# Sparse attention: softmax weights left unscaled, head outputs scaled by reciprocal sums that go through DRAM

## The chip, the cores and the metric

The kernel runs on one core of one Trainium2 chip, as one launch. The metric is the device time of that launch in microseconds. TensorE is PE in the rows below (its weight loads PEld), VectorE is DVE, ScalarE is ACT, GpSimd is POOL, and SyncE is SP, which issues nearly all DMAs in the order in which they stand in its queue. Every engine works through its own instructions in a fixed order and waits on semaphores of the others.

## What is computed

One decoder layer on 512 tokens of width 1024, and a final RMSNorm. Two branches read the same normed input: sparse attention with 16 heads of 64, and a Mamba-2 scan. Both are gated and merged, and a gated MLP follows. The change is in the attention branch, whose core is, for each block of 128 queries:

```python
c_sel = gather(c_kv, sel)                       # the 128 keys that an indexer selected
logits = einsum("bqhc,bqkc->bhqk", qb, c_sel) * scale + bias[t5_bucket(dist)]
p = softmax(where(dist >= 0, logits, -inf), axis=-1)
out = einsum("bhqk,bqkc->bqhc", p, c_sel)       # later, per head:
att = einsum("bshc,hdc->bshd", out, w_uv)
y_att = att.reshape(b, s, 1024) @ w_att_out
```

The kernel doesn't gather: a mask `msk` of 0 and a very negative number picks the selected keys, and all causal keys are computed. A softmax row is exp(logit - max) divided by the sum of its exps. The division may be done on the weights, or on the output of the weighted sum, since it is one number per query and head.

## The kernel before

All tensors stay in SBUF, 128 partitions wide. A float32 matrix is split into a rounded part (`hi`, written by ACT, `split` and L86) and the rest (`lo`, a subtraction, L87), and a product is three matmuls. Weights come as tiles `wr` of 128x1024 through `fetch` (two buffers), ACT makes `wh`, POOL makes `wl` (three buffers each).

The attention stage runs from about 440 to 640 us. Its loop (L852) goes over heads h = 0 to 17. In one turn it emits, for head h, four logit steps `lg(i)`, one per block of 128 queries, with one to four blocks of keys (L764); for head h-2 the product with V (`pav_`); for head h-1 the transposes of its weights (`ptrans`); then the softmax of head h (`soft`). Between these steps `weave` lays the projections as filling work for PE: `pq` and `pk` (query and key of the next pair of heads) in even turns, `pgs` (a gate) in odd ones, and every fourth head the values `pV`. Heads go in pairs, p = h // 2, since two heads of 64 fill 128 partitions.

The steps that matter here, with what they run on:

- `logits` (L743): SP loads `T`, a table of the head's position bias, 128x256 (L748, two buffers). POOL adds it to the mask into `bm` (one buffer): L752, the wide L753, twice L759. So POOL can write `bm` of head h only when DVE has read that of head h-1 in its last logit step.
- `lg(i)`: PE multiplies into a PSUM bank `pl`; DVE adds `bm` and takes the row maximum `mx` (L769).
- `soft`: DVE negates `mx` (L773), ACT computes four exps with their sums `sm` (L776), DVE takes the reciprocal of `sm` (L778) and multiplies the weights `pr` by it, block by block (L781).
- `ptrans`: PE transposes ten blocks of `pr` into three banks `pPT`; ACT writes `PTh` (L800), DVE `PTl` (L801).
- `pav_`: eight matmuls into a bank `pav`. The main part of the product is in the 64 rows `r`, a small part in the other 64, `o_`. ACT copies the small part into `hi` of the pair's tile (L821, named `ath`), SP moves it to the right rows of `lo` (L822, `atl`), DVE copies the main part into `cr` (L823, one buffer per pair).
- `att_split(p)` (L825): adds both parts (L829) and splits the sum into `ath` and `atl` of the pair, for the projection `pao`. The add and the subtraction run on POOL for pairs 0 to 5 and on DVE for pairs 6 and 7.

The banks of `pl`, `pav`, `pPT`, `pV` come from one ring of four PSUM banks (`cht`): a new one waits until the fourth before it has been read. The order in each engine's queue is set by a scheduler of the framework from the emitted program; PE's is close to the emitted order, while ACT, DVE, POOL and SP are ordered by when it expects their inputs. After the loop the kernel goes on with `pga` (another gate) and `pao` (the output projection of attention) by turns, 24 matmuls each, then the rest of the layer, which nothing of the change touches.

Of the kernel before, what the change touches and what calls it, by code (L numbers as in the profile page):

```python
# [9 lines left out]
F32 = mybir.dt.float32  # L10
R32 = mybir.dt.float32r
AF = mybir.ActivationFunctionType
OP = mybir.AluOpType

P = 128
S = 512
NB = S // P
D = 1024
KD = D // P
H = 16  # L20
# [9 lines left out]
SEG = (0, 128, 512, 896)  # L30
# [18 lines left out]
def _body(ctx, tc, x, prm_d, cst_d, nfin_d, wI_d, wX_d, wSO_d, wQ_d, wG_d, wAO_d, wO_d, wUp_d, wDn_d,  # L49
          wkv_d, out):  # L50
    nc = tc.nc
# [6 lines left out]
    dram = enter(tc.tile_pool(name="dram", bufs=1, space=bass.MemoryType.DRAM))  # L58
# [6 lines left out]
    def cht(name):  # L65
        return pc.tile([P, 512], F32, tag="ch", name=name)

    def f(t):
        return t.bitcast(F32)
# [12 lines left out]
    ident = cv("ident")  # L82

    def split(hi, lo, src, lo_eng=None):

        nc.scalar.activation(hi, src, AF.Copy)  # L86
        (lo_eng or nc.vector).tensor_tensor(lo, src, f(hi), OP.subtract)  # L87
# [232 lines left out]
    for t in range(4):  # L320
# [3 lines left out]
        for hh in range(2):  # L324
            h = 2 * t + hh
# [366 lines left out]
            split(hi, lo, raw, lo_eng=nc.gpsimd)  # L692
            wkv.append((hi, lo))

    qTs, kTs, Vs, prs, PTs = {}, {}, {}, {}, {}
    KOF = (0, 512, 1024, 896)

    def v_step(qd):
# [44 lines left out]
    def logits(h):  # L743
        p, hh = h // 2, h % 2
        qh, ql = qTs[p][hh]
        kt = kTs[p][hh]
        T = ap_.tile([P, 256], F32, tag="T", name=f"T{h}")
        nc.sync.dma_start(T, bass.AP(tensor=skD.tensor, offset=skD.offset + h * P * UW + 127,  # L748
                                     ap=[[UW - 1, P], [1, 256]]))
        bm = ap_.tile([P, SEGW], F32, tag="bm", name=f"bm{h}", bufs=1)  # L750
        r31 = pv("r31", h, h + 1)
        nc.gpsimd.tensor_tensor(bm[:, 0:P], msk[:, 0:P], T[:, P:], OP.add)  # L752
        nc.gpsimd.tensor_tensor(  # L753
            bass.AP(tensor=bm.tensor, offset=bm.offset + P, ap=[bm.ap[0], [512, 3], [1, 256]]),
            bass.AP(tensor=msk.tensor, offset=msk.offset + P, ap=[msk.ap[0], [512, 3], [1, 256]]),
            T.unsqueeze(1).to_broadcast([P, 3, 256]), OP.add)
        for i in (2, 3):
            o, n = SEG[i], (i - 1) * P
            nc.gpsimd.tensor_tensor(bm[:, o:o + n], msk[:, o:o + n], r31.to_broadcast([P, n]), OP.add)  # L759
        pr = ap_.tile([P, SEGW], F32, tag="pr", name=f"pr{h}")  # L760
        mx = ap_.tile([P, NB], F32, tag="mx", name=f"mx{h}")
        sm = ap_.tile([P, NB], F32, tag="sm", name=f"sm{h}")

        def lg(i):  # L764
            o, n = SEG[i], (i + 1) * P
            pl_ = cht(f"pl{h}_{i}")[:, :n]
            nc.tensor.matmul(pl_, qh[:, i * P:(i + 1) * P], kt[:, :n], start=True, stop=False)
            nc.tensor.matmul(pl_, ql[:, i * P:(i + 1) * P], kt[:, :n], start=False, stop=True)
            nc.vector.tensor_tensor_reduce(pr[:, o:o + n], pl_, bm[:, o:o + n], 1.0, -3e38, OP.add, OP.max,  # L769
                                           mx[:, i:i + 1])  # L770

        def soft():
            nc.vector.tensor_scalar(mx, mx, -1.0, None, OP.mult)  # L773
            for i in range(NB):
                o, n = SEG[i], (i + 1) * P
                nc.scalar.activation(pr[:, o:o + n], pr[:, o:o + n], AF.Exp, bias=mx[:, i:i + 1],  # L776
                                     accum_out=sm[:, i:i + 1])
            nc.vector.reciprocal(sm, sm)  # L778
            for i in range(NB):
                o, n = SEG[i], (i + 1) * P  # L780
                nc.vector.tensor_scalar(pr[:, o:o + n], pr[:, o:o + n], sm[:, i:i + 1], None, OP.mult)  # L781
            prs[h] = pr

        return [lambda i=i: lg(i) for i in range(NB)] + [soft]

    def ptrans(h):
        pr = prs[h]
        PT = (ap_.tile([P, 1280], R32, tag="PTh", name=f"PTh{h}", bufs=1),
              ap_.tile([P, 1280], R32, tag="PTl", name=f"PTl{h}", bufs=1))
        PTs[h] = PT  # L790

        def one(bk, kbs):
            pt = cht(f"pPT{h}_{bk}")
            w = 0
            for kb in kbs:
                for i in range(kb, NB):
                    nc.tensor.transpose(pt[:, w:w + P], pr[:, SEG[i] + kb * P:SEG[i] + (kb + 1) * P], ident)
                    w += P
            o = KOF[kbs[0]]
            nc.scalar.activation(PT[0][:, o:o + w], pt[:, :w], AF.Copy)  # L800
            nc.vector.tensor_tensor(PT[1][:, o:o + w], pt[:, :w], f(PT[0][:, o:o + w]), OP.subtract)  # L801

        return [lambda a=a: one(*a) for a in enumerate(((0,), (1, 3), (2,)))]

    crs = {}

    def pav_(h):

        p, hh = h // 2, h % 2
        r, o_ = slice(64 * hh, 64 * hh + 64), slice(64 - 64 * hh, 128 - 64 * hh)  # L810
        V, PT = Vs[p // 2], PTs[h]
        pav = cht(f"pav{h}")
        for i in range(2):
            for kb in range(NB):
                o = KOF[kb]
                nc.tensor.matmul(pav[:, kb * P:], V[:, kb, h % 4, :], PT[i][:, o:o + S - kb * P],
                                 start=(kb == 0 and i == 0), stop=(kb == NB - 1 and i == 1))
        hi, lo = attT[p]
        if hh == 0:
            crs[p] = ap_.tile([P, S], F32, tag="cr", name=f"cr{p}", bufs=1)  # L820
        nc.scalar.activation(hi[o_], pav[o_], AF.Copy)  # L821
        nc.sync.dma_start(f(lo[r]), f(hi[o_]))  # L822
        nc.vector.tensor_copy(crs[p][r], pav[r])  # L823

    def att_split(p):  # L825
        hi, lo = attT[p]
        s_ = crs[p]
        eng = nc.vector if p >= 6 else nc.gpsimd
        eng.tensor_tensor(s_, s_, f(lo), OP.add)  # L829
        split(hi, lo, s_, lo_eng=eng)  # L830

    sds.close()
# [19 lines left out]
    for h in range(H + 2):  # L852
        p = h // 2
        fl = []
        if h == 2:
            open_att()
        if h < 2:
            hg = len(gs[0]) // 2
            fl = [so[6 + h]] + gs[0][h * hg:(h + 1) * hg]
        elif h < H:  # L860
            if h % 2 == 0 and p + 1 < 8:
                fl = list(qn[p + 1])
            elif h % 2 == 1:
                fl = list(gs[p])
        chain = []
        lg = logits(h) if h < H else []
        chain += [(i < 3, s_) for i, s_ in enumerate(lg[:NB])]
        if h >= 2:
            chain.append((0, lambda: pav_(h - 2)))
        if 1 <= h <= H:  # L870
            chain += [(i == 1, s_) for i, s_ in enumerate(ptrans(h - 1))]
        if h % 4 == 1 and h < H:
            chain.append((0, v_step(h // 4)))
        chain += [(1, s_) for s_ in lg[NB:]]
        if h >= 5 and h % 2 == 1:
            chain.append((0, lambda: att_split((h - 5) // 2)))
        weave(chain, fl)
# [230 lines left out]
```

## Time and profile before

| what | value |
|---|---|
| median of 3 runs | 1142.02 us (1140.78 to 1142.1) |
| profiled execution, own time | 1139.67 us |
| its span (first to last instruction) | 1137.9 us |
| PE busy | 1094.5 us, 96% of the span |
| DVE busy | 669.2 us, 59% |
| ACT busy | 589.3 us, 52% |
| POOL busy | 504.5 us, 44% |
| granted TensorE clock | 0.995 of full speed (the upper of its two levels, 2.4 GHz) |

PE is busy nearly everywhere, so the span falls only where PE waits or where its work shrinks. Busy shares are means over stages with different limits; the attention stage has to be read by itself. The profiled execution took 1139.67 us, of which 1.8 us lie around the span; it is 2.35 us below the median of the runs.

### The profile page before, as it was taken

What the parts mean: (1) busy time and instruction counts of PE and PEld (TensorE: products, weight loads), DVE (VectorE), ACT (ScalarE), POOL (GpSimd) and SP (SyncE); (2) the same over time, 40 slices, a digit from 0 to 9 for tenths busy, and PEclk for the clock granted to TensorE, in tenths of its full rate; (3) what the DMA queues carried; (4) which work ended last, traced back from release to release, by engine and by line L of the source; (5) the groups of instructions that cost most, each with busy time, mean ns of one, the idle gap of its engine ahead of it and who ended that gap; (6) DMA issues with size and microseconds to landing.
All of it is one profiled execution on the core that took longest, in us unless ns stands there. A gap on an engine that the chain in (4) does not pass through costs nothing.

```text
span 1137.9 us, 14581 instructions
## 1 busy us (share of the span) xinstructions
PE 1094.5 (96%) x5268; PEld 906.7 (80%) x5268; DVE 669.2 (59%) x1340; ACT 589.3 (52%) x948; POOL 504.5 (44%) x279
## 2 busy tenths in 40 slices
PE   5999999999999999899998999999999999999997
PEld 5777778788888887787887888878888888888885
DVE  4589999995696894578889433135344343420004
ACT  5364776687767654366766432244444444431223
POOL 3424334344344345666664344443444444444442
PEclk9999999999999999999999999999999999999999
DMA  5464322323322314434433233323322232223321
GB/s 195 122 192 142 117 93 88 102 91 110 102 94 93 130 58 121 137 89 125 126 98 93 84 130 111 112 84 104 110 93 93 95 108 94 93 93 95 107 96 74
DMA packets 43305, 122.06 MB, mean 107 GB/s; under 512 B 5392, under 2 KB 9760, under 8 KB 43232
## 3 DMA queue, kind: packets, MB, share of 16 engines
q1 hardware_dynamic: 42656, 120.07, 33.2%
q8 instruction: 42, 0.69, 0.2%
q10 hardware_dynamic: 576, 1.05, 0.2%
q14 instruction: 31, 0.25, 0.1%
HBM read 108.29 MB, written 5.32 MB: 100 GB/s over the span
## 4 chain that ended last, share of the span: by engine, by line
PE 66%; DVE 19%; ACT 4%; POOL 3%; issue 3%; DMA 1%; POOLq 0%; DVEq 0%; ACTq 0%
PE pup L112 21%; PE pdn L969 10%; PE pxbc L389 6%; PE pso L480 5%; PE pao L112 4%; PE pga L112 4%; PE pwo L913 4%; DVE msk L349 2%; DVE m L348 2%; DVE u L404 2%; DVE pr L781 2%; DVE pr L769 2%; ACT pr L776 1%; PE pz L455 1%; PE pz L456 1%
## 5 line engine op out<-in xcount | busy, mean ns | idle before, releaser
L87 POOL TENSOR_TENSOR wl<-wr,wh 128x1024 fp32r<-128x1024 f32 x168 | 405.9, 2417 | 506.3 <-ACT wh L86 247.1
L86 ACT ACTIVATE wh<-wr 128x1024 fp32r<-128x1024 f32 x168 | 178.0, 1060 | 216.3 <-PE pdn L969 80.6
L952 DVE SCALAR_TENSOR_TENSOR fu<-pup,prm,fu 128x511 f32<-128x511 f32 x88 | 65.9, 749 | 124.5 <-ACT fu L950 122.9
L112 PE MATMUL pup<-hTh,wh 128*128 128x512 f32 (+1 forms) x368 | 88.0, 381 | 1.6 <-ACT hTh L151 0.8
L112 PE MATMUL pup<-hTl,wh 128*128 128x512 f32 (+1 forms) x368 | 87.7, 380 | 0.0
L112 PE MATMUL pup<-hTh,wl 128*128 128x512 f32 (+1 forms) x368 | 87.5, 380 | 0.0
L112 PEld LDWEIGHTS pup<-hTh,wh 128*128 128x128 f32 x368 | 67.2, 188 | 15.1 <-ACT hTh L151 1.0
L112 PEld LDWEIGHTS pup<-hTl,wh 128*128 128x128 f32 x368 | 67.2, 188 | 13.1
L112 PEld LDWEIGHTS pup<-hTh,wl 128*128 128x128 f32 x368 | 67.2, 188 | 13.1
L969 PE MATMUL pdn<-wl,fh 128*128 128x512 f32 x176 | 68.6, 390 | 1.2 <-POOL wl L87 1.2
L969 PE MATMUL pdn<-wh,fl 128*128 128x512 f32 x176 | 68.5, 389 | 0.0
L969 PE MATMUL pdn<-wh,fh 128*128 128x512 f32 x176 | 68.4, 390 | 0.0
L996 DVE TENSOR_TENSOR x<-pdn,x 128x512 f32<-128x512 f32 x8 | 5.5, 688 | 104.6 <-PE pdn L969 104.6
L404 DVE SCALAR_TENSOR_TENSOR u<-pxbc,prm,u 128x511 f32<-128x511 f32 (+2 forms) x72 | 53.2, 738 | 8.7 <-ACT u L402 8.6
L389 PE MATMUL pxbc<-hTl,wh 128*128 128x512 f32 x192 | 53.5, 402 | 0.0
L455 PE MATMUL pz<-wh,hTh 128*128 128x512 f32 x128 | 51.3, 401 | 1.1 <-DVE u L404 1.1
L389 PE MATMUL pxbc<-hTh,wh 128*128 128x512 f32 x192 | 51.6, 396 | 0.0
L389 PE MATMUL pxbc<-hTh,wl 128*128 128x512 f32 x192 | 50.5, 392 | 0.0
L457 PE MATMUL pz<-wh,hTl 128*128 128x512 f32 x128 | 50.1, 391 | 0.0
L456 PE MATMUL pz<-wl,hTh 128*128 128x512 f32 x128 | 50.0, 391 | 0.0
L950 ACT ACTIVATE fu<-pup,prm 128x512 f32<-128x512 f32 x44 | 34.3, 780 | 27.4 <-PE pup L112 27.4
L776 ACT ACTIVATE pr<-pr,mx 128x128 f32<-128x128 f32 (+1 forms) x64 | 35.5, 557 | 15.3 <-DVE mx L773 15.3
(361 smaller groups left out, 2512.1 us busy)
## 6 DMA issues: line engine op xcount, KB each, us to landing
wr<-wUp SPq DMA_DIRECT2D x44, 512.0 KB, 3.5
wr<-wX SPq DMA_DIRECT2D x40, 512.0 KB, 3.5
wr<-wDn SPq DMA_DIRECT2D x22, 512.0 KB, 3.4
dec<-acD SPq DMA_DIRECT2D x32, 256.0 KB, 3.7
wr<-wSO SPq DMA_DIRECT2D x16, 512.0 KB, 3.5
wr<-wG SPq DMA_DIRECT2D x16, 512.0 KB, 3.7
x<-x SPq DMA_DIRECT2D x8, 512.0 KB, 4.4
wr<-wQ SPq DMA_DIRECT2D x8, 512.0 KB, 3.5
```

Source lines behind the costliest of these rows:

```text
L86: nc.scalar.activation(hi, src, AF.Copy)
L87: (lo_eng or nc.vector).tensor_tensor(lo, src, f(hi), OP.subtract)
L112: nc.tensor.matmul(ps, l, r, start=(i == 0), stop=(i == len(seq) - 1))
L389: nc.tensor.matmul(st["ps"], *st["it"][i], start=(i == 0), stop=(i == 23))
L404: nc.vector.scalar_tensor_tensor(u[:, d:], ps[:, :S - d], pv("cw", o + 3 - d, o + 4 - d), u[:, d:], OP.mult, OP.add)
L455: nc.tensor.matmul(ps, actT[k][0][:, bs], wh[:, ws], start=(k == 0), stop=False)
L456: nc.tensor.matmul(ps, actT[k][0][:, bs], wl[:, ws], start=False, stop=False)
L457: nc.tensor.matmul(ps, actT[k][1][:, bs], wh[:, ws], start=False, stop=(k == KD - 1))
L480: nc.tensor.matmul(ps, *seq[i], start=(i == 0), stop=(i == 11))
L776: nc.scalar.activation(pr[:, o:o + n], pr[:, o:o + n], AF.Exp, bias=mx[:, i:i + 1], accum_out=sm[:, i:i + 1])
L952: nc.vector.scalar_tensor_tensor(u[:, d:], ps[:, :S - d], pv("fw", o + 2 - d, o + 3 - d), u[:, d:], OP.mult, OP.add)
L969: nc.tensor.matmul(po8[b][hf], l[:, bs], r[:, ws], start=(k == 0 and i == 0), stop=(k == NF - 1 and i == 2))
```

## The change

The weights `pr` are no longer scaled. The reciprocal on 128x4 (L778) and the four multiplications (L781) of each head go. Instead the sums of both heads of a pair share one tile of 128x8, and a new function `sums(p)`, emitted in every even turn of the loop after the transposes, lets PE transpose that tile into a bank `psm` of the ring (8x128), DVE take the reciprocal into `si`, and SP write it to a new DRAM tile `smD`. When the second head of a pair has its product, SP reads `smD` back twice, each time one head's 512 numbers repeated over 64 partitions, into `ath`, whose small part has been moved to `atl` by then. `att_split` multiplies by it after the add and before the split, on the same engine. `cr` gets two buffers in place of one, and `T` one in place of two.

```diff
-    qTs, kTs, Vs, prs, PTs = {}, {}, {}, {}, {}
+    qTs, kTs, Vs, prs, PTs, sms = {}, {}, {}, {}, {}, {}
+    smD = dram.tile([H // 2, 2 * NB, P], F32, tag="smD", name="smD")
+
+    def sums(p):
+
+        pt = cht(f"psm{p}")[:2 * NB, :P]
+        nc.tensor.transpose(pt, sms[p], ident)
+        si = ap_.tile([2 * NB, P], F32, tag="si", name=f"si{p}", bufs=1)
+        nc.vector.reciprocal(si, pt)
+        nc.sync.dma_start(smD[p], si)
...
-        T = ap_.tile([P, 256], F32, tag="T", name=f"T{h}")
+        T = ap_.tile([P, 256], F32, tag="T", name=f"T{h}", bufs=1)
...
-        sm = ap_.tile([P, NB], F32, tag="sm", name=f"sm{h}")
+        if hh == 0:
+            sms[p] = ap_.tile([P, 2 * NB], F32, tag="sm", name=f"sm{p}")
+        sm = sms[p][:, hh * NB:(hh + 1) * NB]
...
-            nc.vector.reciprocal(sm, sm)
-            for i in range(NB):
-                o, n = SEG[i], (i + 1) * P
-                nc.vector.tensor_scalar(pr[:, o:o + n], pr[:, o:o + n], sm[:, i:i + 1], None, OP.mult)
...
-            crs[p] = ap_.tile([P, S], F32, tag="cr", name=f"cr{p}", bufs=1)
+            crs[p] = ap_.tile([P, S], F32, tag="cr", name=f"cr{p}", bufs=2)
...
+        if hh == 1:
+            for i in range(2):
+                nc.sync.dma_start(f(hi[64 * i:64 * i + 64]),
+                                  bass.AP(tensor=smD.tensor, offset=smD.offset + (2 * p + i) * S,
+                                          ap=[[0, 64], [1, S]]))
...
         eng.tensor_tensor(s_, s_, f(lo), OP.add)
+        eng.tensor_tensor(s_, s_, f(hi), OP.mult)
...
             chain += [(i == 1, s_) for i, s_ in enumerate(ptrans(h - 1))]
+            if h % 2 == 0:
+                chain.append((0, lambda: sums((h - 1) // 2)))
```

PE's order stays as it was but for one `psm` per pair, right ahead of the three matmuls of `pk`, and for the last two heads. The queues of the other engines change in more places. Three of them follow; the names end in the head (`T5`, `bm4`, `pr3`, `pav1`), in the pair (`ath0`, `cr0`, `kT2`) or in the number of a weight tile (`wh69`), and what stands behind the underscore is a buffer's number.

SP, from the key tiles of pair 2 to the first part of pair 1's `atl`, before:

```order
L731 DMA kT2_1_4873<-kl2_4868 64x512
L822 DMA atl0_4736<-ath0_4735 64x512
L748 DMA T6_5231<-skD_101 128x256
L95 DMA wr71_5479<-wQ 128x1024
L748 DMA T7_5357<-skD_101 128x256
L822 DMA atl1_4738<-ath1_4737 64x512
```

and now:

```order
L704 DMA smD_4285<-si0_4846 8x128
L741 DMA kT2_0_4859<-kl2_4858 64x512
L741 DMA kT2_1_4863<-kl2_4858 64x512
L758 DMA T5_5092<-skD_101 128x256
L830 DMA atl0_4726<-ath0_4725 64x512
L834 DMA ath0_4725<-smD_4285 64x512 x2
L95 DMA wr71_5459<-wQ 128x1024
L758 DMA T6_5214<-skD_101 128x256
```

The second part of `atl0` stood ahead of the next table and now stands behind one, `T5`, whose only buffer `bm4` reads; the two loads of the reciprocals follow it.

POOL, from the end of head 4's `bm` to the start of head 5's, before:

```order
L759 TENSOR_TENSOR bm4_4982<-msk_98,prm_72 128x256
L829 TENSOR_TENSOR cr0_4813<-cr0_4813,atl0_4736 128x512
L87 TENSOR_TENSOR atl0_4736<-cr0_4813,ath0_4735 128x512
L87 TENSOR_TENSOR wl69_5250<-wr69_5247,wh69_5249 128x1024
L752 TENSOR_TENSOR bm5_5108<-msk_98,T5_5106 128x128
```

and now:

```order
L769 TENSOR_TENSOR bm4_4968<-msk_98,prm_72 128x256
L842 TENSOR_TENSOR cr0_4803<-cr0_4803,atl0_4726 128x512
L87 TENSOR_TENSOR wl69_5233<-wr69_5230,wh69_5232 128x1024
L843 TENSOR_TENSOR cr0_4803<-cr0_4803,ath0_4725 128x512
L87 TENSOR_TENSOR atl0_4726<-cr0_4803,ath0_4725 128x512
L762 TENSOR_TENSOR bm5_5094<-msk_98,T5_5092 128x128
```

A weight tile's subtraction moved from behind the pair's two operations to between the add and the new multiplication.

ACT, from head 3's exps to the first exps of head 4, before:

```order
L821 ACTIVATE ath0_4735<-pav1_4924 64x512
L800 ACTIVATE PTh2_4887<-pPT2_0_4936 128x512
L800 ACTIVATE PTh2_4887<-pPT2_1_4943 128x512
L776 ACTIVATE pr3_4884,sm3_4886<-pr3_4884,mx3_4885 128x128
...
L776 ACTIVATE pr3_4884,sm3_4886<-pr3_4884,mx3_4885 128x512
L86 ACTIVATE ath0_4735<-cr0_4813 128x512
L739 ACTIVATE tgs1_4977<-pgs1_4903 128x512
L86 ACTIVATE wh69_5249<-wr69_5247 128x1024
L86 ACTIVATE wh70_5379<-wr70_5377 128x1024
L776 ACTIVATE pr4_4987,sm4_4989<-pr4_4987,mx4_4988 128x128
```

and now:

```order
L788 ACTIVATE pr3_4874,sm1_4750<-pr3_4874,mx3_4875 128x128
L829 ACTIVATE ath0_4725<-pav1_4913 64x512
L808 ACTIVATE PTh2_4876<-pPT2_0_4927 128x512
...
L788 ACTIVATE pr3_4874,sm1_4750<-pr3_4874,mx3_4875 128x512
L86 ACTIVATE wh69_5232<-wr69_5230 128x1024
L749 ACTIVATE tgs1_4963<-pgs1_4892 128x512
L86 ACTIVATE ath0_4725<-cr0_4803 128x512
L86 ACTIVATE wh70_5361<-wr70_5359 128x1024
L788 ACTIVATE pr4_4973,sm2_4975<-pr4_4973,mx4_4974 128x128
```

The copy of `pav1` moved behind the first exps of head 3, and the split of pair 0 (`ath0<-cr0`) from ahead of `wh69` to behind it; the exps of head 4 stand behind that split in both.

## Rows read from the trace of the kernel before

**Rows 1.** Windows: us, then busy us (instructions) of each engine, clock, DMA.

```profile
484.00:605.00 121.00, 118.31 (x636) 99.30 (x635) 103.20 (x246) 83.06 (x195) 77.56 (x67) 1.00 0.42 115
```

**Rows 2.** Waits of PE, 430 to 645 us: total us, times, longest us.

```profile
PE pav L816 <- DVE mx L769: 4.4, 3, 2.7
PE pPT L797 <- DVE pr L781: 2.0, 1, 2.0
```

**Rows 3.** Groups by line: busy us, mean ns | idle before.

```profile
L781 DVE TENSOR_SCALAR pr<-pr,sm 128x128 f32<-128x128 f32 (+1 forms) x64 | 38.7, 654 | 0.5
```

**Rows 4.** Timeline, first head's weights: start us, us, engine, line, [idle before <-releaser].

```profile
476.02 3.50 DVE L781 TENSOR_SCALAR pr<-pr,sm 128x128 f32<-128x128 f32 x4
...
479.57 0.66 PE L797 MATMUL pPT<-cst,pr 128*128 128x128 f32 x4 [1.98 <-DVE pr L781]
```

**Rows 5.** Timeline of POOL, heads 4 and 5.

```profile
501.60 0.46 POOL L752 TENSOR_TENSOR bm<-msk,T 128x128 f32<-128x128 f32 x1 [4.99 <-DVE mx L769]
...
504.75 1.30 POOL L829 TENSOR_TENSOR cr<-cr,atl 128x512 f32<-128x512 f32 x1
...
508.23 2.68 POOL L87 TENSOR_TENSOR wl<-wr,wh 128x1024 fp32r<-128x1024 f32 x1
510.87 0.45 POOL L752 TENSOR_TENSOR bm<-msk,T 128x128 f32<-128x128 f32 x1
```

**Rows 6.** Timeline of POOL, later starts of an even head's `bm`.

```profile
521.41 0.46 POOL L752 TENSOR_TENSOR bm<-msk,T 128x128 f32<-128x128 f32 x1 [4.99 <-DVE mx L769]
...
543.53 0.46 POOL L752 TENSOR_TENSOR bm<-msk,T 128x128 f32<-128x128 f32 x1 [4.99 <-DVE mx L769]
...
605.27 0.46 POOL L752 TENSOR_TENSOR bm<-msk,T 128x128 f32<-128x128 f32 x1 [4.99 <-DVE mx L769]
```

**Rows 7.** Timeline of ACT, from head 3's product to head 4's exps.

```profile
499.90 0.59 ACT L821 ACTIVATE ath<-pav 64x512 fp32r<-64x512 f32 x1
...
506.09 0.64 ACT L86 ACTIVATE ath<-cr 128x512 fp32r<-128x512 f32 x1 [1.77 <-POOL cr L829]
...
508.50 1.06 ACT L86 ACTIVATE wh<-wr 128x1024 fp32r<-128x1024 f32 x1 [0.35 <-PE pq L389]
510.97 0.40 ACT L776 ACTIVATE pr<-pr,mx 128x128 f32<-128x128 f32 x1 [1.40 <-DVE mx L773]
```

**Rows 8.** Timeline of DVE, head 4's scaling.

```profile
516.09 0.41 DVE L781 TENSOR_SCALAR pr<-pr,sm 128x128 f32<-128x128 f32 x1
...
517.26 1.08 DVE L781 TENSOR_SCALAR pr<-pr,sm 128x256 f32<-128x256 f32 x3
```

**Rows 9.** Timeline of SP's queue in the same stretch.

```profile
501.37 0.55 SPq L822 DMA_DIRECT2D atl<-ath  x1
503.90 0.33 SPq L748 DMA_DIRECT2D T<-skD  x1
```

**Rows 10.** DMA issues: KB each, median us to landing.

```profile
dec<-acD SPq DMA_DIRECT2D x32, 256.0 KB, 3.7
...
atl<-ath SPq DMA_DIRECT2D x16, 128.0 KB, 2.4
```

**Rows 11.** Line 259, a reciprocal of 128 numbers per partition: ns min/median/max, start us.

```profile
L259 DVE RECIPROCAL sp_z<-sp_z x1: 954/954/954, 32.9 to 32.9; 128x128 f32<-128x128 f32 x1
```

**Rows 12.** Timeline, head 12's product and head 13's transposes.

```profile
615.50 0.83 PE L816 MATMUL pav<-PTh,V 128*128 128x512 f32 x4 [2.71 <-DVE mx L769]
...
616.80 1.27 PE L797 MATMUL pPT<-cst,pr 128*128 128x128 f32 x10
```

**Rows 13.** Timeline, from the last product to the output projection.

```profile
632.54 0.59 ACT L821 ACTIVATE ath<-pav 64x512 fp32r<-64x512 f32 x1 [1.69 <-PE pav L816]
...
636.16 0.69 DVE L829 TENSOR_TENSOR cr<-cr,atl 128x512 f32<-128x512 f32 x1 [2.31 <-DMA atl<-ath]
636.26 2.03 PE L112 MATMUL pao<-ath,wh 128*128 128x512 f32 x8
...
637.60 2.07 DVE L87 TENSOR_TENSOR atl<-cr,ath 128x512 fp32r<-128x512 f32 x1 [0.74 <-ACT ath L86]
```

## The prediction

> **What bounds the kernel now.** The page comes first: PE is busy 96% of the span at the full clock, so a change pays where it takes away a wait of PE or work of PE. This one touches the attention stage alone, so the next view is the busy time by windows there. Over 121 us of the stage PE is busy 118.3, DVE 103.2, ACT 83.1, POOL 77.6 [rows 1]. PE has 2.7 us of idle time in that stretch, DVE is the next fullest. The list of PE's waits, taken over the whole stage, names DVE: 4.4 us for a row maximum in three waits, the longest 2.7, and 2.0 us in one wait for the scaled weights [rows 2]. The scaling itself is 64 instructions and 38.7 us of DVE, 654 ns in the mean [rows 3]; one case is seen in detail at the first head, where four of them take 3.50 us and PE stands 1.98 us until they are through [rows 4].
>
> So far the change looks like 38.7 us off the engine that PE waits for. But what the stage can give back is the waits, some 7 us, and not the 38.7; and the timeline of POOL shows a second thing. An even head's `bm` starts at 501.60, 521.41 and 543.53, the last such pair of heads begins at 605.27 [rows 5, 6]: intervals of 19.81 us, or 22.12 where the values V are made, five of them in 103.67 us. Each starts when DVE has taken the odd head's maximum. PE fills these intervals nearly wholly [rows 1], so anything that makes the chain from one such start to the next longer than PE's work sets a new pace. The reader should keep that chain in view, since the change lays new links into it.
>
> **What goes.** Per head the reciprocal and four multiplications on DVE. Of this only the waits count: 1.98 us at the first head [rows 4] go wholly, as the transposes then need only the exps, which ACT has finished before PE comes there. I take **-2.0 us**. The other waits on DVE (4.4 us, [rows 2]) would go too if nothing came in their place.
>
> **What comes on PE, DVE and POOL.** Eight transposes of 128x8 on PE: ten transposes took 1.27 us [rows 12], so some 0.13 each and 1.0 in all; below nothing they can't cost. Eight reciprocals on DVE: 128 numbers per partition took 0.954 us at the only such row [rows 11], against 0.17 to 0.2 for the small ones that go. Six multiplications on POOL of the shape of the add, 1.30 us each [rows 5], and two on DVE at 0.69 [rows 13]. On DVE these are small beside what goes.
>
> **The chain between two pairs, step by step.** I take the stretch from 501.60, when POOL starts head 4's `bm`.
>
> (1) *Before*: the second part of pair 0's `atl` was issued at 501.37 [rows 9] and landed 2.4 us later [rows 10], so POOL could add at 504.75, right behind `bm` [rows 5]. *Now* it stands in SP's queue behind `T5`, which has one buffer and must wait until `bm4` has read `T4`: that is the moment at which SP issues a table in the trace, 503.90 [rows 9]. Behind its 0.33 us the part is issued at about 504.3 and lands at 506.7. The add runs from 506.7 to 508.0, two us later than before.
>
> (2) Then POOL takes the weight tile, 2.4 us by the next such row's kind and 2.68 where DVE meets it [rows 5], to 510.4 or 510.7. The two reads of the reciprocals wait until `atl` has landed and follow at 506.8 and 507.4; with the 2.4 us of `atl` they land at 509.8, with the 3.7 us of the other load that repeats DRAM rows over partitions (twice the size) at 511.1 [rows 10]. So they are hidden behind the weight tile, or cost up to 0.5 us; I take them as hidden. The multiplication ends at 511.7 to 512.0.
>
> (3) ACT's split of the pair waits for it (0.64), and a weight copy (1.06) stands next [rows 7]. Only then come the exps of head 4, at 513.4 to 513.7. Before, the split was done at 506.7 and the exps began at 510.97, waiting for DVE alone [rows 7]. That is what the added wait holds up: on ACT the exps, the copy of the next product and with it the release of PSUM banks. The new `psm` takes the fourth bank behind that product, so PE, in order, waits at `psm` until that copy and DVE's have been made.
>
> (4) From the exps to the next interval's start it was 521.41 - 510.97 = 10.44 us [rows 6, 7]. DVE's multiplications of head 4 lie in it, 0.41 + 1.08 [rows 8], and a small reciprocal; the new reciprocal of 0.95 takes their place. I take 9.7 to 9.9.
>
> The sum is 523.1 to 523.6, an interval of 21.5 to 22.0 us against 19.81. Where V is made, the chain is the same (V's matmuls run beside it), against 22.12. I take 21.7: five intervals are 108.5 us against 103.67, **+4.8 us**. Bounds: if `atl` came as early as before, the add, the tile and the multiplication would end at about 509.8 and the interval would fall under PE's own work: nothing lost, and the waits won. If the loads take the 3.7 us and the multiplication waits for them, 22.2 and more, +7.
>
> One rule bears on step 2. DVE and POOL disturb each other in the trace: a weight tile took 2.68 us where DVE worked on SBUF alone beside it [rows 5], and DVE's last subtraction 2.07 us instead of some 0.69 [rows 13]. The Trainium skill (SBUF — State Buffer, "Who interferes with whom") says that of such a pair the second to start is blocked for the whole of the first. By the rule POOL could lose the whole 0.69 us of a DVE instruction per pair and not the 0.27 of the row; the sum would be about 2 us higher. The row is what I go by.
>
> **The last pairs.** At head 12's product PE stood 2.71 us for DVE [rows 12], behind scaling that goes. But the copy of this product stands on ACT behind pair 5's split, which waits for POOL's multiplication as above: by the chain it comes at 605.27 + 11 = 616.3 or a little later, and PE, which has moved the gate's matmuls behind the product, waits at `psm` instead. I take 0, from -2.7 (the wait goes) to +0.5.
>
> At the end the pair must be split before `pao` can go on. Before: copy at 632.54, `atl` landed and added at 636.16, the hi part some 1.4 us later, and PE reached its use 1.6 us into `pao` at 636.26 [rows 13]: just in time. Now the reciprocal (0.95), its write, the two loads (some 0.5 us to issue the second, 2.4 to land) and a multiplication of 0.69 come in between, about 4 us; the scheduler has laid eight matmuls of the next gate ahead of the use, 2.03 us at the rate of [rows 13]. With pair 6's multiplication standing on DVE ahead of head 15's parts (about 0.5) I take **+1.5**, from 0 to 3.
>
> The sum: -2.0 + 4.8 + 0 + 1.5 = **+4.3 us**; the transposes lie in PE's new waits. On the profiled execution that is 1139.67 + 4.3 = 1144.0. That execution lay 2.35 us under the median of the runs, so for the median 1142.02 + 4.3 = **1146.3 us**.
>
> **The rivals.**
>
> *A. PE stays the bound* (the other side). If the chain closes within PE's work, at 20 us or less, by a table that SP issues earlier or an add that doesn't wait, all waits of [rows 2] go: 2.0 + 4.4, less 1.0 for the transposes; and at the end of the stage +1.0 at most remains. About -4.5: 1137.5 us. For it: DVE loses 38.7 us of work, and all links of the chain have had slack so far (POOL waited 4.99 us ahead of three of its starts, [rows 5, 6]). Against it: step 1 and step 3 are the order of the queues. It decides where the interval falls below 20.4 us.
>
> *B. The two cancel.* With an interval of 21.1 us, 0.6 less per pair than I take (a load that lands a little earlier, DVE's row maxima ready sooner), five intervals cost +1.8, and with -2.0 and +1.0 it is within 0.2%: about 1142.5.
>
> *C. DRAM is slow.* The reads follow a write of the same DRAM tile and repeat one row 64 times. At the 3.7 us of [rows 10] and more, the multiplication waits for them, some +1 per pair and +2 at the end: 1152 or more.
>
> **How the numbers follow.** What a measurement of this kernel can tell from no change is about 0.2%, 2.3 us. Forecast (own range 1144.3 to 1151): 0.47. A: 0.20. B: 0.25. C: 0.08. Slower is the forecast and C, 0.55; same is B, 0.25; faster is A, 0.20. The range reaches from A's time to the top of the forecast, 1137.5 to 1151; it leaves out C and the better half of A.
>
> **What would show it.** Right: DVE's busy time falls by some 30 us; PE's list of waits has `psm` waiting for DVE's copy `cr`, 1 to 2 us per pair, in place of the waits of [rows 2]; the starts of `bm` of heads 4, 6, 8 lie about 21.7 us apart whether V is made or not; ACT waits for POOL's multiplication ahead of the split of each pair; `pao`'s eighth matmul or the DVE multiplication ahead of it waits for the load of `ath`. Wrong: intervals of 20 us and below without V, or PE dense at `psm`; then the chain had room and A holds. If the multiplication waits for the load and not for POOL's own queue, C holds.

## The result and the profile after

The changed kernel takes 1149.55 us (median of 4 runs, 1144.82 to 1151.2), the kernel before, run beside it, 1141.83. The ratio is 1.0064 with a 95% interval of 1.0042 to 1.0086: slower by about 7 us. The forecast was 1146.3 in a range of 1137.5 to 1151, slower with a chance of 0.55. The profiled execution took 1149.65 us (span 1147.9), 9.98 more than the profiled one of before.

Busy times of the engines, from the page of the changed kernel:

```profile
PE 1099.6 (96%) x5276; PEld 912.6 (80%) x5276; DVE 646.2 (56%) x1270; ACT 587.1 (51%) x948; POOL 512.2 (45%) x285
```

DVE lost 23 us of work, as meant, and POOL gained 8. The time is in PE's waits, in the view that [rows 2] show of before (total us, times, longest us; 430 to 655 us):

```profile
PE psm L701 <- DVE cr L831: 11.4, 7, 3.0
...
PE pPT L805 <- DVE mx L781: 1.2, 1, 1.2
```

The waits of [rows 2] on the scaled weights and on most row maxima are gone. In their place PE stands 11.4 us at `psm`, seven times, up to 3.0 us each, until DVE has copied a product out of the bank that `psm` takes. The starts of an even head's `bm` on POOL, which [rows 5, 6] show of before:

```profile
498.05 0.45 POOL L762 TENSOR_TENSOR bm<-msk,T 128x128 f32<-128x128 f32 x1 [4.06 <-DVE mx L781]
...
519.59 0.46 POOL L762 TENSOR_TENSOR bm<-msk,T 128x128 f32<-128x128 f32 x1 [3.36 <-DVE mx L781]
...
541.99 0.46 POOL L762 TENSOR_TENSOR bm<-msk,T 128x128 f32<-128x128 f32 x1 [3.36 <-DVE mx L781]
...
565.39 0.46 POOL L762 TENSOR_TENSOR bm<-msk,T 128x128 f32<-128x128 f32 x1 [4.22 <-DVE mx L781]
...
609.90 0.46 POOL L762 TENSOR_TENSOR bm<-msk,T 128x128 f32<-128x128 f32 x1 [4.19 <-DMA wr<-wG]
```

The intervals are 21.54, 22.40 and 23.40 us and then 22.24 and 22.27 (one start, 587.63, is left out), whether V is made in them or not; five are 111.85 us against 103.67. The longest of them, step by step. SP, POOL, ACT and PE from 541.99 on:

```profile
544.27 0.35 SPq L758 DMA_DIRECT2D T<-skD  x1
544.71 0.46 SPq L830 DMA_DIRECT2D atl<-ath  x1
545.26 3.87 SPq L834 DMA_DIRECT2D ath<-smD  x2
```

```profile
548.82 1.29 POOL L842 TENSOR_TENSOR cr<-cr,atl 128x512 f32<-128x512 f32 x1 [3.65 <-DMA atl<-ath]
550.07 2.39 POOL L87 TENSOR_TENSOR wl<-wr,wh 128x1024 fp32r<-128x1024 f32 x1
552.42 1.28 POOL L843 TENSOR_TENSOR cr<-cr,ath 128x512 f32<-128x512 f32 x1
```

```profile
553.74 0.63 ACT L86 ACTIVATE ath<-cr 128x512 fp32r<-128x512 f32 x1 [5.96 <-POOL cr L843]
554.28 1.04 ACT L86 ACTIVATE wh<-wr 128x1024 fp32r<-128x1024 f32 x1
555.22 0.39 ACT L788 ACTIVATE pr<-pr,mx 128x128 f32<-128x128 f32 x1
```

```profile
557.58 0.27 PE L701 MATMUL psm<-cst,sm 128*8 128x128 f32 x1 [3.01 <-DVE cr L831]
```

The reader is to see the chain close: the table, then `atl`, then (4.1 us later) the add, the weight tile, the multiplication, ACT's split with 5.96 us of waiting before it, the weight copy, the exps, the copy of the product, and PE at `psm`. POOL doesn't wait between add, tile and multiplication: the reads of the sums are hidden behind the tile.

### The profile page after: what moved, and what is told of

It reads as the page before. It is cut to its first block, busy times and chain, and to the rows that moved or that the text cites. A ratio compares the mean times of both kernels' runs of the same rounds, so it can differ in the third digit from the quotient of the medians.

```text
span 1147.9 us, 14577 instructions
## 1 busy us (share of the span) xinstructions
PE 1099.6 (96%) x5276; PEld 912.6 (80%) x5276; DVE 646.2 (56%) x1270; ACT 587.1 (51%) x948; POOL 512.2 (45%) x285
## 4 chain that ended last, share of the span: by engine, by line
PE 70%; DVE 16%; ACT 3%; POOL 3%; DMA 2%; issue 2%; POOLq 0%; ACTq 0%; DVEq 0%; SPq 0%
PE pup L112 21%; PE pdn L985 10%; PE pxbc L389 6%; PE pso L480 5%; PE pao L112 4%; PE pwo L929 3%; PE pga L112 3%; PE pgs L389 3%; DVE msk L349 2%; PE pq L389 2%; DVE m L348 2%; DVE u L404 2%; POOL wl L87 1%; PE pz L456 1%; PE pz L455 1%
## 5 line engine op out<-in xcount | busy, mean ns | idle before, releaser
L112 PEld LDWEIGHTS pup<-hTl,wh 128*128 128x128 f32 x368 | 67.7, 190 | 13.1
L112 PEld LDWEIGHTS pup<-hTh,wl 128*128 128x128 f32 x368 | 67.3, 188 | 13.1
```

The lines of the kernel that those rows point to most:

```text
L112: nc.tensor.matmul(ps, l, r, start=(i == 0), stop=(i == len(seq) - 1))
```

## The experiments

Each run was timed beside the kernel before. The third column is the sum of the five intervals between the starts of an even head's `bm` (heads 4 to 14) in the run's own trace, the last the time from one early `pq` matmul to one late `pao` matmul, against the kernel before: the attention stage without the scatter of what lies ahead of it, which was up to 2.7 us. Both columns come from one profiled execution of each kernel.

| run | median us | ratio to before (95%) | five intervals, us | stage, us |
|---|---|---|---|---|
| before | 1141.8 | 1 | 103.67 | 0 |
| changed | 1149.55 | 1.0064 (1.0042 to 1.0086) | 111.85 | +9.7 |
| no_mult | 1137.69 | 0.9965 (0.9951 to 0.9980) | 102.52 | -3.5 |
| psm_other_ring | 1148.92 | 1.0063 (1.0044 to 1.0083) | 109.54 | +8.0 |
| two_T_one_cr | 1150.97 | 1.0088 (1.0056 to 1.0119) | 112.12 | +10.3 |
| no_scaling | 1136.45 | 0.9948 (0.9928 to 0.9968) | 101.33 | -4.2 |
| atl_own_queue | 1137.09 | 0.9964 (0.9945 to 0.9983) | 104.87 | -1.6 |
| all_on_dve | 1145.72 | 1.0028 (1.0016 to 1.0039) | 109.10 | +4.7 |
| all_on_dve_own_tile | 1147.41 | 1.0055 (1.0038 to 1.0072) | 110.25 | +7.5 |
| scale_at_the_copy | 1141.43 | 0.9998 (0.9986 to 1.0011) | 104.14 | -0.1 |
| tables_by_pool | 1144.13 | 1.0017 (1.0003 to 1.0032) | 105.07 | +2.4 |
| before_atl_own_queue | 1146.41 | 1.0038 (1.0023 to 1.0052) | 104.45 | +4.7 |
| atl_own_queue_own_tile | 1139.63 | 0.9981 (0.9965 to 0.9996) | 103.38 | -2.0 |
| atl_own_queue_one_read | 1173.63 | 1.0274 (1.0250 to 1.0297) | 126.38 | +33.9 |

### The multiplication alone

```diff
         eng.tensor_tensor(s_, s_, f(lo), OP.add)
-        eng.tensor_tensor(s_, s_, f(hi), OP.mult)
         split(hi, lo, s_, lo_eng=eng)
```

> The changed kernel without the multiplication of L843 (the outputs stay unscaled); transposes, reciprocals, the write and both reads of the sums stay, and every queue keeps its order. Theory (the chain of a pair, POOL's added 1.3 us on it, ACT's split and with it the exps and the copy of the product behind it): the intervals between even heads' bm, 21.5 to 23.4 us in the changed kernel's trace, fall by 1.3 us each, PE's wait at psm falls from 11.4 us to 3 to 5, and the time by 6 to 9 us, to 1141 to 1144. Rival 'bank' (psm waits since it takes a bank of the ring, whatever POOL does): the time falls by 1 to 2 us at the end of the stage and no more, 1147 to 1149. Rival 'loads' (the reads of the sums from DRAM are what is waited for): ACT's split overwrites what they read into and still waits for them, so the time stays at 1149.

It came to 1137.69 us, lower than expected, and PE's wait at `psm` fell to 3.2 us. Its wait lists (PE over 430 to 660 us, ACT over 480 to 625):

```profile
PE psm L701 <- DVE cr L831: 3.2, 4, 1.7
...
ACT ath L86 <- DMA ath<-smD: 12.8, 6, 3.4
```

Taking one POOL instruction per pair off the chain takes 9.3 us off five intervals: the 1.3 us each that it lasts (1.76 in one of the five), 6.9 in all, and 2.4 more, of which the fall of the clock behind PE's waits (below) is a part. ACT's split now does wait for the reads of the sums, 2.1 us on average, and that costs nothing: transposes, write and reads fit under PE's work by themselves. The rivals 'bank' and 'loads' both fall.

### Where the wait shows

```diff
-        pt = cht(f"psm{p}")[:2 * NB, :P]
+        pt = mmt(f"psm{p}")[:2 * NB, :P]
```

> The changed kernel with psm in the ring of the projections' banks instead of the ring of pl, pav and pPT. Theory (chain): the copy cr comes as late as before and pl of the next head takes the bank in its place, so PE's wait moves from psm to pl, behind the three matmuls of pk (0.85 us): the time falls by 2 to 5 us, to 1144 to 1147, and the intervals stay over 21 us. Rival 'bank': the wait of 11.4 us at psm goes and nothing takes its place, 1138 to 1140.

```profile
PE pl L779 <- DVE cr L831: 5.1, 5, 1.4
PE pav L824 <- ACT ath L86: 1.8, 1, 1.8
```

The wait moved to `pl`, as the theory had it, and the time stayed (1148.92): the 2 to 5 us that I expected on top didn't come, the intervals stayed at 21.5 to 22.5. So `psm` is only the place where PE meets the chain; a bank from another ring buys nothing that the medians show.

### Buffers or the order of the queue

```diff
-        T = ap_.tile([P, 256], F32, tag="T", name=f"T{h}", bufs=1)
+        T = ap_.tile([P, 256], F32, tag="T", name=f"T{h}")
-            crs[p] = ap_.tile([P, S], F32, tag="cr", name=f"cr{p}", bufs=2)
+            crs[p] = ap_.tile([P, S], F32, tag="cr", name=f"cr{p}", bufs=1)
```

> The changed kernel with the buffers of the kernel before: T two, cr one. SP's queue then has T8 where it had T7 ahead of the second part of a pair's atl, and T8 waits for the same reader (bm6) as T7 did with one buffer. Theory (the order of SP's queue, not the number of buffers): no change, 1147 to 1151. Rival (T's one buffer is what holds atl up): atl lands 2 us earlier, intervals of 20 us, 1140 to 1144.

No change, as expected: 1150.97, intervals 112.12. The numbers of buffers of `T` and `cr`, which the change sets, are not what costs. With two tables, the scheduler only lays the table after the next one into the same place.

### Nothing in place of the scaling

```diff
-            nc.vector.reciprocal(sm, sm)
-            for i in range(NB):
-                o, n = SEG[i], (i + 1) * P
-                nc.vector.tensor_scalar(pr[:, o:o + n], pr[:, o:o + n], sm[:, i:i + 1], None, OP.mult)
```

> The kernel before with the scaling left out and nothing in its place (the weights stay unnormalised). SP's and POOL's queues take nearly the order of the changed kernel: the next table ahead of the second part of atl, the weight tile ahead of the pair's subtraction. Theory: the add comes 2 us later than before, but ACT's split follows it at once, so the chain of a pair stays under PE's work; the waits of PE for DVE go (4.4 + 2.0 us): 1134 to 1138, intervals 19.8 to 20.2 us. Rival (the new order of the queues costs by itself, with no multiplication): intervals over 21 us and 1142 or more.

1136.45: this is all that the DVE work of [rows 3] can give back, some 6 us of 38.7. And this kernel's queues have the later table ahead of `atl` (issued at 541.94 and 542.37) and the tile ahead of the subtraction (546.29 and 549.12) too: the new order, by itself, fits under PE's work, with five intervals of 101.33 us. It takes the order and the multiplication together to make the chain too long.

### The order of SP's queue

```diff
-        nc.sync.dma_start(f(lo[r]), f(hi[o_]))
+        nc.scalar.dma_start(f(lo[r]), f(hi[o_]))
```

> The changed kernel with the DMAs of the small part (ath to atl) issued by ACT, right behind its copy, instead of by SP, where they stand behind the next table. The scheduler then lays POOL's multiplication ahead of the weight tile. Theory (the order of the queues is what makes the chain long): the add comes 2 to 4 us earlier, ACT's split 2.4 us, the intervals between even heads' bm (21.5 to 23.4 us in the changed kernel's trace) fall to 20 to 20.8 us, PE's wait at psm from 11.4 us to under 4, the time to 1140 to 1144. Rival (the added operations by themselves are what is too long): intervals over 21 us, 1147 or more.

1137.09 us, better than the 1140 to 1144 expected, and 12 us under the changed kernel, though its intervals, 21.0 us in the mean, are longer than the 20 to 20.8 expected. Of the 11.3 us that its stage is shorter, 7.0 lie in the five intervals and 3.8 behind head 14. ACT issues the DMA 0.1 us after the start of the interval, not 2.7 (the interval begins at 539.36; ACT and ACT's queue, then POOL):

```profile
538.87 0.59 ACT L829 ACTIVATE ath<-pav 64x512 fp32r<-64x512 f32 x1 [1.45 <-PE pav L824]
539.49 0.49 ACTq L830 DMA_DIRECT2D atl<-ath  x1
...
548.63 0.63 ACT L86 ACTIVATE ath<-cr 128x512 fp32r<-128x512 f32 x1 [2.21 <-POOL cr L843]
```

```profile
544.47 1.31 POOL L842 TENSOR_TENSOR cr<-cr,atl 128x512 f32<-128x512 f32 x1 [1.91 <-DMA atl<-ath]
547.30 1.30 POOL L843 TENSOR_TENSOR cr<-cr,ath 128x512 f32<-128x512 f32 x1 [1.52 <-DMA ath<-smD]
```

The split comes 9.3 us into the interval and not 11.8. But three orders changed in this run: SP's; with it POOL's (the tile no longer stands between add and multiplication); and ACT's, where the copy of the product stands ahead of the first exps again, 0.5 us ahead of the interval's start and not 0.7 behind it. The next run changes SP's alone.

```diff
-        nc.sync.dma_start(T, bass.AP(tensor=skD.tensor, ...
+        nc.gpsimd.dma_start(T, bass.AP(tensor=skD.tensor, ...
```

> The changed kernel with the position tables T issued by POOL instead of SP. SP's queue then has both parts of atl ahead of nothing that waits for bm, while POOL keeps its order, a weight tile between add and multiplication. It tells apart the two orders that changed together in the run with atl on ACT's queue. Theory (SP's order): the multiplication ends 2 to 3 us earlier, intervals 20 to 21 us, 1141 to 1145, most of what that run gained. Rival (POOL's order, the weight tile ahead of the multiplication): intervals stay over 21.3 us, 1147 or more.

```profile
543.42 0.40 ACT L788 ACTIVATE pr<-pr,mx 128x128 f32<-128x128 f32 x1 [3.00 <-DVE mx L785]
...
543.94 0.59 ACT L829 ACTIVATE ath<-pav 64x512 fp32r<-64x512 f32 x1
```

```profile
544.56 0.46 SPq L830 DMA_DIRECT2D atl<-ath  x1
```

```profile
547.15 1.30 POOL L842 TENSOR_TENSOR cr<-cr,atl 128x512 f32<-128x512 f32 x1 [0.24 <-DMA atl<-ath]
548.59 2.41 POOL L87 TENSOR_TENSOR wl<-wr,wh 128x1024 fp32r<-128x1024 f32 x1
550.96 1.76 POOL L843 TENSOR_TENSOR cr<-cr,ath 128x512 f32<-128x512 f32 x1
```

The interval shown begins at 543.21, `atl` is issued 1.35 us into it, the tile still stands in between, and the intervals are 20.36, 21.97, 20.38, 21.97 and 20.39: 105.07 in all, nearly the 104.87 of atl_own_queue, and longer where V is made, as in the kernel before. So it is SP's order that carries the loop, 6.8 of the 8.2 us that the intervals had lost; POOL's order and ACT's together give no more than 0.2 on top. ACT's is not nothing for the issue of `atl`, though. In the kernel before it came 0.23 us ahead of the interval's start [rows 5, 9], in the changed kernel 2.7 behind it; the table's place makes 1.36 of these 2.95 us, and the other 1.6 come with the copy's new place behind the exps, which this run keeps. Only the table had to go to bring the chain back near PE's work. This run's stage is still 4.0 us longer than that of atl_own_queue, 1.7 of it up to head 4 and 2.1 behind head 14; the rest of the 7 us between their medians isn't in the stage of the profiled executions, and I leave it open.

Is it the queue alone that gains? The same edit in the kernel before:

> The kernel before with the DMAs from ath to atl issued by ACT, and nothing else changed: what the other queue is worth without the change. Theory: the chain of a pair had room in the kernel before and PE waited for DVE (4.4 and 2.0 us), so it stays within 0.2%, 1140 to 1144. Rival (the queue is the whole gain of the run with atl on ACT's queue): 1136 to 1138.

It is slower, 1146.41, which I had not expected. Its intervals are nearly those of before; from head 14 on it loses 4.2 us, where PE waits 3.5 us for DVE at the transposes of head 13 and 1.9 us at `pao`. So the gain of atl_own_queue is not the queue's alone: with the DMA on ACT's queue the change is worth 9 us (1146.41 to 1137.09), and 5 against the kernel before as it was (1142.46, timed beside it).

### Are the reads of the sums what is waited for

```diff
-        eng = nc.vector if p >= 6 else nc.gpsimd
+        eng = nc.vector
```

> The changed kernel with the add, the multiplication and the subtraction of all eight pairs on DVE (0.69 us each) and none on POOL. Theory: the split no longer waits behind a weight tile of 2.4 us on POOL; the small part still lands late, and the loads of the sums wait for it: intervals 20.2 to 21 us, 1141 to 1145. Rival 'loads': DVE's multiplication waits for the loads of the sums as long as POOL's did for its tile, intervals as in the changed kernel, 1147 or more.

1145.72, a little above what was expected, intervals 109.10. `atl` is as late as in the changed kernel (issued 2.7 us into the interval), and the multiplication stands in DVE's queue behind row maxima and the gate's product `ys`, which took 2.68 us at 505.31, beside POOL's weight tile. DVE did wait for the reads, in two of six pairs, 2.0 us in all. The same with the sums read early, into a tile of their own:

```diff
...
+        bcs[p] = ap_.tile([P, S], F32, tag="bc", name=f"bc{p}", bufs=1)
+        for i in range(2):
+            nc.sync.dma_start(bcs[p][64 * i:64 * i + 64], ...
...
-        eng.tensor_tensor(s_, s_, f(hi), OP.mult)
+        eng.tensor_tensor(s_, s_, bcs[p], OP.mult)
```

> As the run with all on DVE, and the sums are read from DRAM into a tile of their own (cr has one buffer to make room), as soon as they are written, and not into ath after the small part has left it. Theory: where the loads are hidden this is the same time within 1.5 us. Rival 'loads': 2 to 4 us less than with the loads into ath, since multiplication and split then wait for DVE alone.

1147.41 us, not faster. But it isn't a clean test of the reads: SP issues them ahead of `atl`, which so goes out 3.9 us into the interval (546.15, from 542.24) and not 2.7, and in pairs 0, 2 and 4 DVE makes `ys` (2.52 us at 548.06) ahead of the add. That is likely why it is slower by 1.7 us; it also has one `cr` in place of two, and no run takes these apart. Against the reads as the limit speak no_mult, and POOL in the changed kernel, which never waited for them. The own tile on top of atl_own_queue:

> The changed kernel with atl issued by ACT and the sums read into a tile of their own (one cr) as soon as they are written. POOL's order is then add, multiplication, subtraction, weight tile. In the run with atl on ACT's queue POOL waited 7.2 us in four waits for the loads of the sums and ACT 8.9 us for the multiplication. Theory: both go, the intervals (19.7 to 22.1 us there) fall to 20 to 21 us, 1134 to 1137, the best of all. Rival (PE's work is the bound there already): the same as that run, 1136 to 1139.

1139.63, not below 1137.09. POOL's waits for the reads didn't go (7.9 us in six waits): SP issues the early reads behind the same table. The rival, that PE's own work is the bound there (1136 to 1139), stands nearer, but isn't shown.

### Another place for the scaling

```diff
...
-        nc.scalar.activation(hi[o_], pav[o_], AF.Copy)
+        nc.vector.tensor_tensor(hi[o_], pav[o_], bcs[h][o_], OP.mult)
...
-        nc.vector.tensor_copy(crs[p][r], pav[r])
+        nc.vector.tensor_tensor(crs[p][r], pav[r], bcs[h][r], OP.mult)
```

> A version with the sums broadcast through DRAM but no operation added behind the small part's move: per head the reciprocals of 128x4 (DVE), a transpose, a copy (ACT), a write, one read repeated over 128 partitions into a tile of its own, and both copies out of the product's bank become multiplications by it on DVE (the one that ACT made too). The pair's add and split are as in the kernel before. Theory: the chain is that of the kernel with no scaling (intervals 19.7 to 21.1 us there), and PE has eight more transposes than the changed kernel: 1136 to 1141, faster than both kernels. Rival (DRAM's round trip per head is too long, the product's copies wait for it): PE waits for DVE's multiplications behind the read, intervals over 21 us, 1145 or more.

1141.43, the time of the kernel before and just above the 1136 to 1141 expected: the loop holds (104.14), but PE waits 5.4 us at seven of its sixteen `psm`, now for DVE's `PTl`, and the end of the stage takes back 3.5 us.

### The last run

On top of atl_own_queue, and with `psm` in the other ring:

```diff
...
-            for i in range(2):
-                nc.sync.dma_start(f(hi[64 * i:64 * i + 64]), ... ap=[[0, 64], [1, S]]))
+            nc.sync.dma_start(f(hi), ... ap=[[S, 2], [0, 64], [1, S]]))
```

> The run with atl on ACT's queue (3 us of PE's waits at psm and 7.2 us of POOL's waits for the two loads of the sums are left in it), with the two loads made one DMA over 128 partitions, and psm in the ring of the projections' banks. Theory: with the chain of a pair now just above PE's work, a load that ends some 0.5 us earlier and a PE that doesn't wait at psm take 1 to 3 us off: 1134 to 1136.5. Rival (PE's own work is the bound there): the same as that run within 1 us, 1136 to 1138.

1173.63 us: the opposite of what I expected. POOL's waits (480 to 660 us):

```profile
POOL cr L841 <- DMA ath<-smD: 31.0, 5, 6.6
```

One of the DMAs is issued at 553.78, and the multiplication that reads what it brings starts at 561.08. Windows of one us in between (last two columns: share of 16 DMA engines, GB/s):

```profile
556.00:557.00 1.00, 1.00 (x7) 0.88 (x6) 0.04 (x2) 0.00 (x0) 0.00 (x0) 1.00 0.13 49
557.00:558.00 1.00, 1.00 (x6) 0.82 (x5) 0.57 (x2) 0.00 (x0) 0.00 (x0) 1.00 0.14 53
558.00:559.00 1.00, 1.00 (x7) 0.80 (x5) 0.00 (x0) 0.00 (x0) 0.00 (x0) 1.00 0.13 49
559.00:560.00 1.00, 1.00 (x9) 0.95 (x7) 0.87 (x3) 0.00 (x0) 0.00 (x0) 1.00 0.13 49
```

A share of 0.13 is two of 16 engines, for six us. The Trainium skill (DMA: Bandwidth & Descriptors, "Why a DMA increments its semaphore by 16 and not by 1") says that a DMA runs on the largest number of engines, up to 16, that divides the slowest dimension of both its patterns; for a pattern that begins with a two that is two, and the trace agrees. So this run says little of the bank, which changed with it, but it shows rival C at work: where the read does take 7 us in place of 3, five intervals take 126 us.

## Why the prediction was right, and where its sizes were off

The mechanism on record is the one that the runs show: a chain of one pair's steps that closes behind PE's work, made longer by SP's order and by one POOL operation, with PE standing at `psm`. It was worked out from the order of the queues and from the durations of before. By its steps, in us from the start of an interval:

| step | predicted | pair 0 (498.05) | pair 1, with V | pair 2 (541.99) | pair 3, with V | pair 4 |
|---|---|---|---|---|---|---|
| second part of `atl` issued | 2.7 | 2.7 | 2.7 | 2.7 | 2.7 | 2.7 |
| add starts | 5.1 | 5.3 | 6.2 | 6.8 | 5.3 | 5.2 |
| multiplication ends | 10.1 to 10.4 | 10.7 | 11.5 | 11.7 | 10.7 | 10.6 |
| exps of the even head | 11.8 to 12.1 | 12.2 | 13.1 | 13.2 | 12.9 | 12.1 |
| next start | 21.5 to 22.0 | 21.5 | 22.4 | 23.4 | 22.2 | 22.3 |

For pair 0 it is nearly to the point, partly by luck: its exps came 0.1 to 0.4 us later than predicted, and the last step took 9.3 us where step 4 has 9.7 to 9.9. By parts of the span, in the profiled executions:

| part | predicted | found |
|---|---|---|
| ahead of the stage, no edit | 0 | -0.83 |
| stage up to head 4 | -2.0 | -2.72 |
| five intervals | +4.8 | +8.18 |
| from head 14 to `pao` | 0 and +1.5 | +4.27 |
| behind the stage, no edit | 0 | +1.08 |
| sum | +4.3 | +9.98 |

The sum was too small: +4.3, where the medians show +7.7 and the profiled executions +10. The range still held the time, but its upper end was set by slow loads, which the changed kernel didn't have; what filled it were the terms below.

**What goes** was right: -2.7 up to head 4, where the wait of [rows 4] is gone.

**Steps 1 and 2** took 2.4 us for the landing of `atl`. That was the median of [rows 10]; in pairs 1 and 2 the add started 3.5 and 4.1 us after the issue, against 2.5 to 2.6 in the other three of the table; why the transfer landed later there no run shows. The weight tile took up to 2.86 us, and two of six multiplications 1.73 and 1.76 in place of 1.30. In pair 3, which has one of these two, the exps waited 0.53 us more for DVE's row maxima: there the chain on POOL had slack, and the interval is close to the 22.12 that V takes in the kernel before. The average interval was 22.4 in place of 21.7: the term of the loop was mis-sized by 3.4 us.

**A missing term: the clock.** In the kernel before the granted clock was 1.00 over the whole stage (its longest part in [rows 1]). In the changed kernel PE stood 3.01 us until 557.58, and then:

```profile
558.00:559.00 1.00, 0.92 (x6) 0.68 (x5) 1.00 (x3) 1.00 (x4) 1.00 (x3) 1.00 0.13 12
559.00:560.00 1.00, 1.00 (x5) 0.83 (x5) 1.00 (x2) 1.00 (x4) 1.00 (x1) 0.67 0.67 199
560.00:561.00 1.00, 1.00 (x4) 0.81 (x3) 1.00 (x3) 0.98 (x2) 1.00 (x1) 0.50 0.73 182
561.00:562.00 1.00, 1.00 (x4) 0.81 (x4) 0.94 (x3) 0.65 (x2) 0.17 (x1) 0.50 0.00 0
562.00:563.00 1.00, 1.00 (x5) 0.86 (x4) 0.94 (x4) 0.00 (x0) 0.00 (x0) 0.62 0.85 127
563.00:564.00 1.00, 1.00 (x6) 0.82 (x5) 0.88 (x4) 0.00 (x0) 0.00 (x0) 1.00 0.80 291
```

A clock of 0.50 is 1.2 GHz (columns: us, busy us of PE, PEld, DVE, ACT, POOL, clock, DMA share, GB/s). The missing parts of these windows add up to 1.7 us of PE's work. The same follows the waits until 602.09 (1.87 us) and 636.94 (1.83 us): three stretches, 5 us of PE's work. In the loop it is partly taken back, since the chain goes on beside PE: the next wait at `psm` was 0.53 us. From the exps to the next start it was 10.2 us in pairs 2 and 4, which hold two of these stretches, and 9.3 to 9.4 in pairs 0, 1 and 3: some 0.8 us of each interval. The +1.08 behind the stage goes with a fourth fall (0.50 in the window 778 to 780, behind waits of 0.4 to 0.8 us at the norm ahead of the MLP), which the profiled execution of before didn't have at that place; no edit reaches there. No term of mine stood for the clock.

**The last pairs.** I had 0 for head 12 and +1.5 for the last, and took `pao` as the place. `pao` waited 0.33 us only. What was lost lies ahead of it, in DVE's queue (DVE, then POOL, then PE):

```profile
633.18 2.50 DVE L750 SCALAR_TENSOR_TENSOR ys<-tgs,ys 128x512 f32<-128x512 f32 x1 [0.61 <-ACT tgs L749]
635.61 0.68 DVE L843 TENSOR_TENSOR cr<-cr,ath 128x512 f32<-128x512 f32 x1
636.21 0.67 DVE L831 COPY cr<-pav 64x512 f32<-64x512 f32 x1
...
645.67 2.16 DVE L843 TENSOR_TENSOR cr<-cr,ath 128x512 f32<-128x512 f32 x1 [2.07 <-DMA ath<-smD]
```

```profile
632.75 2.39 POOL L87 TENSOR_TENSOR wl<-wr,wh 128x1024 fp32r<-128x1024 f32 x1 [7.22 <-ACT wh L86]
644.90 2.39 POOL L87 TENSOR_TENSOR wl<-wr,wh 128x1024 fp32r<-128x1024 f32 x1 [9.77 <-PE pga L112]
```

```profile
636.94 0.27 PE L701 MATMUL psm<-cst,sm 128*8 128x128 f32 x1 [1.83 <-DVE cr L831]
```

DVE's instruction at 633.18 lasts 2.50 us, 0.69 where nothing is beside it: it started behind POOL's tile and ended 0.5 us after it. Behind it stand pair 6's multiplication and the copy that frees the bank for `psm`, and PE waits 1.83 us. Here the rule that the prediction weighed (the Trainium skill, SBUF — State Buffer, "Who interferes with whom": the second of such a pair is blocked for the whole of the first) describes the trace better than the row I went by, and on the other engine: I had priced it on POOL, where the tile kept its 2.39 us, and it was DVE that stood still, 1.8 us here and 1.5 at 645.67. No run removes these two, so what they cost at the end of the stage rests on this reading alone.

**The rivals.** A, PE stays the bound, did not occur; the step against it in the prediction, the order of SP's queue, is what decided. The time of atl_own_queue, 1137.09, is A's 1137.5, but not by A's road: its intervals are 21.0 us in the mean, over the 20.4 that A asked for, and PE still waits up to 1.1 us in them. B asked for intervals of 21.1; that is the mean of tables_by_pool (21.0), which is 1144.13. C didn't occur in the changed kernel, where POOL never waited for the reads.

**Its signs.** PE at `psm` behind `cr`, the same interval with V and without, ACT waiting ahead of each split: all there, and at the end DVE's multiplication waits for the load of `ath` (2.07 us at 645.67). That V makes no difference holds in the mean, 22.3 us with it and 22.4 without; in pair 3 the chain on POOL isn't what set it. DVE's fall was 23 us, not 30: the line of `ys<-tgs,ys` took 6.2 us more than before, beside POOL's tiles.

## What to carry to other kernels

An engine that the bound engine waits for 7 us can give back 7 us, whatever work is taken off it; look first at which chain closes a period of the loop, and add the new links to that chain. Where a scheduler sets the queues, read what the change moved in the queue of the engine that issues the DMAs: here one transfer behind one waiting table cost 6.8 us in five intervals, and one word, the engine that issues the transfer, turned 0.6% slower into 0.4% faster than the kernel before (0.9945 to 0.9983). A wait of PE costs more than its length if the clock falls behind it, as in three places here.

## What the runs showed of the hardware that I had not expected

- PE's clock fell to 1.2 GHz behind waits of 1.8 to 3.0 us, and each time that took 1.7 us of PE's work, though PE was busy again at once. It didn't behind each: 1.96 us of waiting until 512.60 left it at 1.00. The changed kernel's fastest run (1144.82 us) had a mean clock of 0.993, the other three (1149.44 to 1151.2) 0.990.
- A DMA of 256 KB whose pattern begins with a two used two of 16 DMA engines and held its reader back for 7 us, where two DMAs of 128 KB each land in 2.9 us (median in the changed kernel).
- A reciprocal of 128 numbers on 8 partitions costs DVE 0.935 us, as the one on 128 partitions of [rows 11]; the 128x4 ones that went cost 0.177.
